# Expert weights stored in pairs and loaded a pair at a time, and the residual's rows loaded straight into their tiles

## The chip, the cores and the metric

The kernel runs on one core of a Trainium2 chip. The metric is device time in microseconds (us) from one run of the whole program; smaller is better. The core's engines are named as in the profile: PE (TensorE, matrix products), PEld (its weight loads), DVE (VectorE), ACT (ScalarE), POOL (GpSimd), SP (SyncE, which here issues nearly all DMAs). SPq in a row is the SP queue that issues DMAs.

## The reference

A small network on 512 tokens of width 1024, all in fp32: a transformer layer with attention and an MLP, a recurrent layer with an MLP, and a third layer with a token mixer and a mixture of experts. The change touches the end of it:

```python
x = x + g1 * token_mixer(h, ...)             # ends with merged @ w_out
h = rms_norm(x, norm2_g) * (1.0 + sc2) + sh2
x = x + g2 * hier_moe(h, ...)                # 32 experts, each token takes 2
return rms_norm(x, final_g)
# one expert on a block of tokens:
(silu(xb @ w_gate[e]) * (xb @ w_up[e])) @ w_down[e]      # 1024 -> 256 -> 1024
```

All 32 experts' weights are read whatever the routing is: 32 x 6 pieces ("units") of 128 x 1024 fp32, 512 KB each, 100.7 MB.

## The kernel before

**Stages.** The program runs the layers one after the other. Weights of the dense layers come through the tile pool `wr` (5 tiles of 512 KB) and are split into a high and a low part in the pool `wh` (4 tiles of 1 MB). A pool of 44 tiles of 128 x 512 (256 KB, `s2`) serves everything else. The last two stages matter here. `output_and_route` multiplies the merged token mixer `M` by `w_out` (the tiles `wo`; the second half of `w_out` stays in the four `wh` tiles `W` until token tile t = 3 is done), adds the residual, normalises (`norm`), writes the rows to DRAM (`h2d`, token tiles 0 to 2 from POOL, t = 3 from SP), and finds each token's experts (`pick`, `table`, `to_index`, which writes `idx`). `experts` then runs 17 blocks: 16 blocks `b` that hold 64 rows of expert b and 64 rows of expert b + 16, and one block "x" of 128 rows for the first expert with more than 64 tokens. For each block POOL gathers the rows (`xg<-h2d,idx`), PE transposes them (`xT`), multiplies by the gate and up weights (`gu`, units 0 to 3 of the expert) and by the down weights (`y`, units 4 and 5), and POOL scatters the result to DRAM (`yd`). At the end the results are read back (`yl`) and added.

**The ring.** Expert weights are loaded ahead into a ring of 33 units that reuses every free buffer: 4 units in own tiles (`wx`, 512 KB), 5 in `wr` tiles, 16 in pairs of `s2` tiles, 8 in the four `wh` tiles. A unit in one piece is one DMA with rows of 4 KB (line 2272); a unit in two `s2` tiles is two DMAs of 256 KB, "halves", with rows of 2 KB (line 2275). `ahead(n)` issues the next n units; `next_w` hands out a unit and calls `ahead(1)`. The calls before the first block are `ahead(4)`, `ahead(8)`, `ahead(9)` and `ahead(12)`. A load waits until the last reader of its buffer is done. All these loads stand in one in-order SP queue, in the order of the ring. Each DMA of the SP queue signals one of eight semaphores in turn and waits for the DMA eight places before it, so that at most eight are in flight.

**The residual.** The rows of the residual lie in DRAM (`xtok`). In `output_and_route` they are loaded to eight `s2` tiles `xt` (line 1860); `residual` multiplies `wo` by the gate into the old tiles `h` and adds `xt`.

```python
if x is not None:
    load = queue.dma_start(out=x, in_=src)                      # L2272: 128 x 1024
else:
    for h in range(2):
        load = queue.dma_start(out=halves[h], in_=src[:, h * 512:(h + 1) * 512])   # L2275: 128 x 512
```

Of the kernel before, what the change touches and what calls it, by code (L numbers as in the profile page):

```python
# [10 lines left out]
F32 = mybir.dt.float32  # L11
F32R = mybir.dt.float32r
# [3 lines left out]
ALU = mybir.AluOpType  # L16
# [4 lines left out]
NT = 4  # L21
# [23 lines left out]
class K:  # L45
# [1412 lines left out]
    def token_mixer(self, X):  # L1458
        nc, A = self.nc, self.A
# [32 lines left out]
        qt, kt, V, kcv = {}, {}, {}, {}  # L1492
# [318 lines left out]
    def open_moe(self):  # L1811
        nc = self.nc
        self.ctxb.close()
        self.c1 = self.ctx.enter_context(self.tc.tile_pool(name="c1", bufs=1))
        self.xg = [self.c1.tile([128, 1024], F32, name=f"xg{i}") for i in range(2)]
        for x in self.xg:
            nc.gpsimd.memset(x, 0.0)
        self.last_add = None
        self.raw, self.unit, self.last_load, self.pair = deque(), 0, None, None


        self.blocks = list(range(13)) + ["x"] + list(range(13, 16))

        def units(b, us):
            return [("x", u) for u in us] if b == "x" else [96 * j + 6 * b + u for u in us for j in range(2)]
# [24 lines left out]
    def output_and_route(self, M):  # L1850

        nc, A = self.nc, self.A
        self.moe_consts()
        g1 = self.row_bcast(self.modrow[0:1])
        self.router()
        xt = {}
        for g in range(2):
            for t in range(NT):
                xt[g, t] = self.s2("xt")
                nc.sync.dma_start(out=xt[g, t], in_=self.xtok[t, :, g * 512:(g + 1) * 512])  # L1860
        self.x2 = self.h
# [20 lines left out]
        for kb in range(4):  # L1882
            w = self.load_w(A["w_out"][0, kb], 1024)
# [258 lines left out]
    def block_rows(self, ov, idx, weight, sel=None):  # L2142


        nc = self.nc
        V = nc.vector
        pos, flag, wf = self.t([128, 8], "ovp"), self.t([128, 8], "ovm"), self.t([128, 2], "ovw")
        V.tensor_scalar(out=pos, in0=self.pe, scalar1=ov[:, 1:2], scalar2=None, op0=ALU.subtract)
        V.tensor_scalar(out=wf[:, 0:1], in0=ov[:, 0:1], scalar1=-1.0, scalar2=None, op0=ALU.add)
        V.tensor_scalar(out=flag, in0=self.ek, scalar1=wf[:, 0:1], scalar2=None, op0=ALU.is_equal)  # L2150
        V.tensor_scalar(out=wf[:, 0:1], in0=wf[:, 0:1], scalar1=0.0, scalar2=1536.0, op0=ALU.max, op1=ALU.mult)
        V.scalar_tensor_tensor(out=idx[:, 2:3], in0=self.io128, scalar=2.0, in1=wf[:, 0:1], op0=ALU.mult, op1=ALU.add)
# [12 lines left out]
        self.to_index(ps[:, 0:2], idx[:, 0:2])  # L2165
        self.shares(ps[:, 2:4], weight)
# [62 lines left out]

        return rows, first, turn, second  # L2230

    def unit_tile(self, m, name="wx"):

        m %= self.NWX + self.NWR + self.NWY + 2 * self.NWH
        if m < self.NWX:
            x = self.c1.tile([128, 1024], F32, name=name, tag="wx", bufs=self.NWX)
        elif m < self.NWX + self.NWR:
            x = self.wp.tile([128, 1024], F32, name=name, tag="wr", bufs=self.NWR)
        elif m < self.NWX + self.NWR + self.NWY:
            return None, [self.s2(name) for _ in range(2)]  # L2240
        else:
            n = (m - self.NWX - self.NWR - self.NWY) % 2
            if n == 0:
                self.pair = self.wp.tile([128, 2, 1024], F32R, name="wh", tag="wh", bufs=self.NWH).bitcast(F32)
            x = self.pair[:, n]
        return x, [x[:, 0:512], x[:, 512:1024]]

    def unit_rows(self, idx, u, halves):

        for h in range(2):  # L2250
            self.nc.gpsimd.indirect_dma_start(out=halves[h], out_offset=None,
                                              in_=self.A["moe_w"].rearrange("u p (h c) -> (u p h) c", h=2),
                                              in_offset=bass.IndirectOffsetOnAxis(ap=idx, axis=0),
                                              element_offset=u * 128 * 1024 + h * 512)
        return halves

    def ahead(self, n, queue=None):

        queue = queue or self.nc.sync
        for _ in range(n):  # L2260
            if self.unit == len(self.order):
                return
            u, (x, halves) = self.order[self.unit], self.unit_tile(self.unit)
            self.raw.append(halves)
            self.unit += 1
            if isinstance(u, tuple):
                self.unit_rows(self.xidx[:, 2:3], u[1], halves)
                continue
            src = self.A["moe_w"][u]
            with self.tc.issue_after(self.last_load) if self.last_load is not None else nullcontext():  # L2270
                if x is not None:
                    load = queue.dma_start(out=x, in_=src)  # L2272
                else:
# [4 lines left out]
    def next_w(self):  # L2278
        w = self.raw.popleft()
        self.ahead(1)  # L2280
        return w
# [20 lines left out]
    def experts(self):  # L2302
        nc, A, tc = self.nc, self.A, self.tc
# [13 lines left out]
        for b in self.blocks:  # L2317
            p = 16 if b == "x" else b
            row = self.xidx[:, 1:2] if b == "x" else self.idx[:, 16 + p:17 + p]
            done = (lambda y: last.update(y=y)) if b == self.blocks[-1] else (lambda y, row=row: put(row, y))  # L2320
            T.append(self.block_tasks(xg[len(T) % 2], ((0, 128),) if b == "x" else ((0, 64), (64, 128)),
                                      self.share[:, p:p + 1], self.next_w, done, len(T) >= n - 2))

        def fetch(i):
            b = self.blocks[i]
# [147 lines left out]
        nc.sync.dma_start(out=self.h[c], in_=self.A["xT"][c])  # L2473

    def run(self):
        self.NS2, self.NWR, self.NWH, self.NWX, self.NWY = 44, 5, 4, 4, 16
        self.AHEAD = 2
        self.open()
        self.open_a()
# [41 lines left out]
def layout(inp):  # L2521
# [129 lines left out]
```

## Time and profile before

| | us |
|---|---|
| median of 3 runs | 2326.76 (2326.37 to 2333.84) |
| the profiled execution, its own time | 2335.61 |
| its span, first to last instruction | 2333.8 |
| PE busy | 2193.7 (94%) |
| DVE busy | 1287.8 (55%) |
| ACT busy | 941.1 (40%) |

The profiled execution took 8.85 us longer than the median, and 1.8 us of its time lie outside its span. Shares over the whole span say little about the two last stages: the stretch from 2010 us to the end is read by windows, by the SP queue's timeline and by waits.

### The profile page before, as it was taken

To read this page: it belongs to the slowest core of one execution; us is meant where nothing else is said; L and a number is where in the kernel's file an instruction comes from. 1 tells how busy PE (TensorE), PEld (TensorE's weight loads), DVE (VectorE), ACT (ScalarE), POOL (GpSimd) and SP (SyncE) were. 2 spreads that over 40 slices of the span, in tenths; PEclk is the share of its full clock that TensorE was granted. 3 is DMA by queue.
4 is the path that set the end of the run, shared out by engine and by line. 5 is a ranking of instruction groups with operands and counts; after the bars stand their busy time and mean duration, and the time that the engine had idled before them with its cause. 6 is when DMAs were issued, how large, how long until landed. Compare 5 with 4: busy or idle time off the path is not lost.

```text
span 2333.8 us, 32061 instructions
## 1 busy us (share of the span) xinstructions
PE 2193.7 (94%) x12050; PEld 1707.5 (73%) x12050; DVE 1287.8 (55%) x2341; ACT 941.1 (40%) x1788; POOL 365.1 (16%) x390
## 2 busy tenths in 40 slices
PE   7999989999998999899999999899999999799886
PEld 5887887866888877878888899787878878633232
DVE  7566487564449779572444476614366655433224
ACT  5445653323234457453322345225257762311111
POOL 4001006122005132210000031200400001111211
PEclk9999999999999999999999999999999999799998
DMA  5211255654333421352223323654620015899996
GB/s 184 65 59 55 96 186 175 208 171 156 127 99 115 140 73 59 98 194 88 99 92 135 100 65 110 208 150 153 230 67 28 2 52 196 285 381 392 375 348 243
DMA packets 153045, 353.52 MB, mean 151 GB/s; under 512 B 31809, under 2 KB 43073, under 8 KB 152888
## 3 DMA queue, kind: packets, MB, share of 16 engines
q1 hardware_dynamic: 146696, 338.45, 42.8%
q0 software_dynamic: 6192, 13.00, 1.5%
q8 instruction: 96, 1.57, 0.3%
q14 instruction: 61, 0.50, 0.1%
HBM read 322.66 MB, written 39.84 MB: 155 GB/s over the span
## 4 chain that ended last, share of the span: by engine, by line
PE 50%; DMA 7%; DVE 6%; ACT 2%; issue 2%; SPq 1%; POOL 0%; ACTq 0%; DVEq 0%; POOLq 0%
PE mm L206 24%; PE mm L232 7%; PE gu L2193 3%; DMA wx<-in_moe_w_dram 3%; PE wo L1868 2%; PE O L1758 2%; PE S L533 2%; PE PT L587 2%; DMA wh<-in_moe_w_dram 2%; PE y L2193 1%; DVE wh L167 1%; PE mm L209 1%; DVE xc L907 1%; PE hps L1607 1%; SPq L1302 1%
## 5 line engine op out<-in xcount | busy, mean ns | idle before, releaser
L167 DVE TENSOR_TENSOR wh<-wr,wh 128x1024 fp32r<-128x1024 f32 x262 | 335.8, 1284 | 437.5 <-ACT wh L164 424.1
L164 ACT CAST wh<-wr 128x1024 fp32r<-128x1024 f32 x274 | 286.9, 1049 | 543.4 <-PE mm L206 394.5
L206 PE MATMUL mm<-xmh,wh 128*128 128x512 f32 x896 | 287.0, 398 | 12.1 <-ACT relu L386 12.1
L206 PE MATMUL mm<-hidh,wh 128*128 128x512 f32 x896 | 287.1, 399 | 4.0 <-DVE m L399 2.1
L206 PEld LDWEIGHTS mm<-xmh,wh 128*128 128x128 f32 x896 | 169.6, 190 | 53.6 <-ACT relu L386 15.6
L206 PEld LDWEIGHTS mm<-hidh,wh 128*128 128x128 f32 x896 | 168.9, 189 | 46.5 <-ACT wh L164 2.5
L206 PE MATMUL mm<-hidl,wh 128*128 128x512 f32 x448 | 179.4, 400 | 0.0
L206 PE MATMUL mm<-xml,wh 128*128 128x512 f32 x448 | 177.6, 396 | 0.0
L206 PE MATMUL mm<-x2h,wh 128*128 128x512 f32 x512 | 168.0, 400 | 2.4 <-ACT cmpY L1481 1.6
L631 PE MATMUL mm<-x0h,wh 128*128 128x512 f32 x384 | 128.3, 404 | 12.5 <-ACT wh L164 9.6
L2193 PE MATMUL gu<-wx,xT 128*64 128x512 f32 (+1 forms) x412 | 120.0, 621 | 13.6 <-DMA wx<-in_moe_w_dram 9.7
L206 PEld LDWEIGHTS mm<-x2h,wh 128*128 128x128 f32 x512 | 96.3, 189 | 22.4 <-ACT cmpY L1481 2.7
L2226 DVE SCALAR_TENSOR_TENSOR y<-y,share,g 128x512 f32<-128x512 f32 x34 | 25.4, 750 | 144.7 <-PE y L2193 136.5
L568 ACT ACTIVATE P<-S,nm 128x128 f32<-128x128 f32 (+3 forms) x192 | 100.5, 535 | 9.6 <-DVE nm L563 9.4
L267 POOL TENSOR_TENSOR sq<-sq 128x512 f32<-128x512 f32 x12 | 17.9, 1488 | 541.5 <-ACT sq L259 541.2
L206 PE MATMUL mm<-x2l,wh 128*128 128x512 f32 x256 | 101.8, 398 | 0.0
L232 PE MATMUL mm<-xgh,wh 128*128 128x256 f32 x512 | 96.4, 288 | 4.6 <-DVE wh L167 4.6
L206 PEld LDWEIGHTS mm<-hidl,wh 128*128 128x128 f32 x448 | 84.9, 189 | 20.7 <-issue 2.8
L206 PEld LDWEIGHTS mm<-xml,wh 128*128 128x128 f32 x448 | 85.1, 190 | 19.4 <-issue 2.3
L631 PEld LDWEIGHTS mm<-x0h,wh 128*128 128x128 f32 x384 | 73.0, 191 | 28.7 <-ACT wh L164 9.6
L2193 PEld LDWEIGHTS gu<-wx,xT 128*64 128x64 f32 (+1 forms) x412 | 32.9, 143 | 80.3 <-issue 44.4
L590 ACT COPY PTs<-PT 128x512 f32<-128x512 f32 (+3 forms) x128 | 63.5, 528 | 63.1 <-PE PT L587 62.6
(551 smaller groups left out, 4807.7 us busy)
## 6 DMA issues: line engine op xcount, KB each, us to landing
wx<-in_moe_w_dram SPq DMA_DIRECT2D x186, 256.0 KB
wr<-in_mlp_up_dram SPq DMA_DIRECT2D x64, 512.0 KB
wr<-in_mlp_down_dram SPq DMA_DIRECT2D x64, 512.0 KB
wx<-in_moe_w_dram SPq DMA_DIRECT2D x52, 512.0 KB
wr<-in_ada_w_dram SPq DMA_DIRECT2D x48, 512.0 KB
wh<-in_moe_w_dram SPq DMA_DIRECT2D x47, 512.0 KB
wr<-in_win_dram SPq DMA_DIRECT2D x40, 512.0 KB
wr<-in_attn_w_dram SPq DMA_DIRECT2D x24, 512.0 KB
```

The source lines that it names most:

```text
L164: nc.scalar.copy(out=wh[:, 0, cs], in_=w)
L167: (lo or nc.vector).tensor_tensor(out=wh[:, 1, cs], in0=w, in1=wh[:, 0, cs].bitcast(F32), op=ALU.subtract)
L206: nc.tensor.matmul(out=ps[j], lhsT=wh[:, b, o:o + 128], rhs=X[k][a], start=st, stop=sp)
L232: mm = nc.tensor.matmul(out=out, lhsT=keep[kb][:, b, o:o + 128], rhs=X[k][a][:, HALF[hf]], start=(k == 0 and n == 0 and j % 2 == 0), stop= ...
L533: nc.tensor.matmul(out=ps, lhsT=q[:, qs], rhs=part[:, 0:N], start=part is k[0], stop=False)
L568: nc.scalar.activation(out=p[:, ns], in_=ps[:, ns], func=AF.Exp, bias=nm[:, o + n:o + n + 1], accum_out=ss[:, o + n:o + n + 1])
L587: nc.tensor.transpose(out=pt[:, c:c + 128], in_=blk[:, kb * 128:(kb + 1) * 128], identity=self.ident)
L590: nc.scalar.copy(out=sb[:, 0:len(part) * N], in_=pt[:, 0:len(part) * N])
L631: nc.tensor.matmul(out=ps, lhsT=w[:, b, k * 128:(k + 1) * 128], rhs=X[k][a], start=(k == 0 and n == 0), stop=(k == 7 and n == 2))
L1758: nc.tensor.matmul(out=oo(e), lhsT=V[kb][:, tp * 256 + g * 64:tp * 256 + (g + 1) * 64], rhs=T[2 * m + e][kb], start=False, stop=(tp == 1 a ...
L1868: nc.tensor.matmul(out=ps, lhsT=M[k][a][:, t * 128:(t + 1) * 128], rhs=w[:, b, kk:kk + 512], start=(k == 0 and n == 0), stop=(k == 7 and n ...
L2193: nc.tensor.matmul(out=out[a:b], lhsT=x[:, c * 128 + a:c * 128 + b], rhs=u[n], start=start, stop=stop)
```

## The change

The weights lie in DRAM as 96 pairs: piece u of expert e and of expert e + 16 side by side, so that a partition's row of a pair is 8 KB. The ring counts in pairs and has 17 (34 units). Where the room is one piece of 1 MB (two new `wx` tiles, the four `wh` tiles) a pair is one DMA; a pair in two `wr` tiles is two DMAs with rows of 4 KB, a pair in four `s2` tiles is four with rows of 2 KB, and the pair called `mix` takes one `wr` and two `s2` tiles. All three read from rows of 8 KB now. The order of the ring is written out. The residual's rows are loaded straight into the tiles `h` (now `x2`), right behind the last use of `h` in `token_mixer`; `residual` writes the product to an `s2` tile `gated` and adds it. The eight `xt` tiles and their loads go. In the block "x" the row index is worked out with two more small DVE operations.

```diff
@@ token_mixer
         self.drain(self.soon)
+        self.x2 = self.h
+        for g in range(2):
+            for t in range(NT):
+                nc.sync.dma_start(out=self.x2[2 * t + g], in_=self.xtok[t, :, g * 512:(g + 1) * 512])
@@ output_and_route
-        xt = {}
-        for g in range(2):
-            for t in range(NT):
-                xt[g, t] = self.s2("xt")
-                nc.sync.dma_start(out=xt[g, t], in_=self.xtok[t, :, g * 512:(g + 1) * 512])
...
             x = self.x2[2 * t + g]
-            nc.vector.tensor_tensor(out=x, in0=ps, in1=g1[g], op=ALU.mult)
-            nc.vector.tensor_tensor(out=x, in0=x, in1=xt[g, t], op=ALU.add)
+            y = self.s2("gated")
+            nc.vector.tensor_tensor(out=y, in0=ps, in1=g1[g], op=ALU.mult)
+            nc.vector.tensor_tensor(out=x, in0=x, in1=y, op=ALU.add)
...
-        self.ahead(self.NWX)
+        self.ahead(2)
...
-        self.ahead(self.NWR + 3)
+        self.ahead(5)
...
-                self.ahead(9)
+                self.ahead(8)
             norm(t)
...
-        self.ahead(self.NWY - 12 + 2 * self.NWH)
+        self.ahead(len(self.RING) - 15)
@@ the ring
+    RING = ("wx",) * 2 + ("wr",) * 2 + ("s2",) * 3 + ("wh",) * 4 + ("s2",) * 5 + ("mix",)
...
+        if kind in ("wx", "wh"):
+            pool, bufs, dt = (self.c1, 2, F32) if kind == "wx" else (self.wp, self.NWH, F32R)
+            x = pool.tile([128, 2, 1024], dt, name=kind, tag=kind, bufs=bufs)
+            x = x if dt == F32 else x.bitcast(F32)
+            return [(x, slice(0, 2), slice(0, 1024))], [[x[:, j, 0:512], x[:, j, 512:1024]] for j in range(2)]
+        for j in range(2):
+            if kind == "wr" or (kind, j) == ("mix", 0):
+                x = self.wp.tile([128, 1024], F32, name="wr", tag="wr", bufs=self.NWR)
+                parts.append((x, j, slice(0, 1024)))
...
+            else:
+                halves.append([self.s2("wx") for _ in range(2)])
+                parts.extend((x, j, slice(h * 512, (h + 1) * 512)) for h, x in enumerate(halves[-1]))
@@ ahead
-            src = self.A["moe_w"][u]
+            src = self.A["moe_w"][6 * b + u]
...
-                if x is not None:
-                    load = queue.dma_start(out=x, in_=src)
-                else:
-                    for h in range(2):
-                        load = queue.dma_start(out=halves[h], in_=src[:, h * 512:(h + 1) * 512])
+                for x, j, cs in parts:
+                    load = self.nc.sync.dma_start(out=x, in_=src[:, j, cs])
@@ layout
-    A["moe_w"] = w.reshape(192, 128, 1024)
+    A["moe_w"] = np.ascontiguousarray(w.reshape(2, 96, 128, 1024).transpose(1, 2, 0, 3))
```

What the change does to the order of the SP queue is seen in three places.

The first is the end of `output_and_route`, up to the load of `g`. `wx`, `wr` and `wh` from `in_moe_w_dram` are expert weights, the size is that of the tile, `h2d` is the write of the rows of t = 3, `g` a gate row. Before:

```order
L1860 DMA xt<-xtok 128x512 x8
L2272 DMA wx<-in_moe_w_dram 128x1024 x4
L2275 DMA wx<-in_moe_w_dram 128x512 x24
L1908 DMA h2d<-h_17936 128x512
L1908 DMA h2d<-h_17937 128x512
L2275 DMA wx<-in_moe_w_dram 128x512 x8
L2272 DMA wh<-in_moe_w_dram 128x1024 x8
L2332 DMA g_18055<-modrow 128x1024
```

Now:

```order
L2282 DMA wr<-in_moe_w_dram 128x1024 x3
L2282 DMA wx<-in_moe_w_dram 128x512 x12
L2282 DMA wh<-in_moe_w_dram 128x2048 x4
L2282 DMA wx<-in_moe_w_dram 128x512 x16
L1908 DMA h2d<-h_17946 128x512
L1908 DMA h2d<-h_17947 128x512
L2282 DMA wx<-in_moe_w_dram 128x512 x4
L2282 DMA wr<-in_moe_w_dram 128x1024
L2282 DMA wx<-in_moe_w_dram 128x512 x2
L2347 DMA g_18051<-modrow 128x1024
```

The `xt` loads are gone. The four `wh` loads, which can start only as the matmuls of t = 3 release the second half of `w_out`, have moved from behind the `h2d` write to before it, and sixteen halves stand between them and the write.

The second is the stage before, where the residual's rows are loaded now (`h` tiles; `cw` are weights of another part). Before:

```order
L1591 DMA cw_14184<-in_cmp_w_dram 128x512
L1591 DMA cw_14186<-in_cmp_w_dram 128x512
L153 DMA wr<-in_win_dram 128x1024 x7
L153 DMA wr<-in_nsa_wo_dram 128x1024
L1620 DMA w_14302<-in_cmp_w_dram 128x256
```

Now:

```order
L1595 DMA cw_14184<-in_cmp_w_dram 128x512
L1595 DMA cw_14186<-in_cmp_w_dram 128x512
L1548 DMA h_86<-xtok 128x512
L1548 DMA h_93<-xtok 128x512
L1548 DMA h_100<-xtok 128x512
L1548 DMA h_107<-xtok 128x512
L1548 DMA h_91<-xtok 128x512
L1548 DMA h_98<-xtok 128x512
L1548 DMA h_105<-xtok 128x512
L1548 DMA h_109<-xtok 128x512
L153 DMA wr<-in_win_dram 128x1024 x7
```

Eight loads of 256 KB stand before the seven loads of `win`.

The third is the end of the loads (`ovd` is a write of a list, `fg` and `yl` serve the last sum). Before:

```order
L2275 DMA wx<-in_moe_w_dram 128x512 x22
L2138 DMA ovd<-ov 128x14x2
L2275 DMA wx<-in_moe_w_dram 128x512 x10
L2272 DMA wh<-in_moe_w_dram 128x1024 x8
L2417 DMA fg<-in_final_g_dram 128x512 x2
L2424 DMA yl<-yd 128x512 x16
```

Now:

```order
L2282 DMA wx<-in_moe_w_dram 128x512 x12
L2282 DMA wh<-in_moe_w_dram 128x2048
L2138 DMA ovd<-ov 128x14x2
L2282 DMA wh<-in_moe_w_dram 128x2048 x3
L2282 DMA wx<-in_moe_w_dram 128x512 x12
L2432 DMA fg<-in_final_g_dram 128x512 x2
L2439 DMA yl<-yd 128x512 x16
```

Behind `ovd` stood ten halves and eight units in `wh`; now three pairs in `wh` and twelve halves. The last three pairs, the last block's, come in rows of 2 KB, where they came in rows of 4 KB.

## Rows read from the trace of the kernel before

**Rows 1.** The page: the span; GB/s in 40 slices; one issue row, last column us to landing.

```profile
span 2333.8 us, 32061 instructions
...
GB/s 184 65 59 55 96 186 175 208 171 156 127 99 115 140 73 59 98 194 88 99 92 135 100 65 110 208 150 153 230 67 28 2 52 196 285 381 392 375 348 243
...
h2d<-h POOLq DMA_DIRECT2D x6, 256.0 KB, 2.9
```

**Rows 2.** Busy time, then TensorE clock, DMA share and GB/s, by stretch.

```profile
1990.00:2010.00 20.00, 20.00 (x121) 17.24 (x120) 5.98 (x20) 8.36 (x20) 2.44 (x4) 1.00 0.61 203
2010.00:2020.00 10.00, 8.14 (x45) 6.91 (x43) 6.11 (x38) 5.74 (x13) 1.08 (x2) 0.90 0.97 363
2020.00:2030.00 10.00, 2.64 (x11) 2.37 (x11) 8.26 (x52) 1.05 (x3) 1.10 (x1) 0.50 0.94 292
...
2044.00:2292.00 248.00, 224.56 (x940) 79.66 (x936) 75.19 (x203) 38.82 (x97) 41.07 (x41) 0.97 1.01 373
2270.00:2280.00 10.00, 10.00 (x48) 3.17 (x46) 2.80 (x6) 1.17 (x4) 0.07 (x1) 1.00 0.77 125
```

**Rows 3.** The same in four 5 us windows of the expert stage.

```profile
2065.00:2070.00 5.00, 4.71 (x22) 1.63 (x24) 2.06 (x10) 1.07 (x3) 0.00 (x0) 1.00 1.04 389
...
2095.00:2100.00 5.00, 5.00 (x25) 1.66 (x22) 1.49 (x3) 0.00 (x0) 0.00 (x0) 1.00 1.03 409
...
2165.00:2170.00 5.00, 4.51 (x17) 1.25 (x16) 0.00 (x0) 0.00 (x0) 0.00 (x0) 1.00 0.89 277
...
2225.00:2230.00 5.00, 1.96 (x7) 0.47 (x6) 0.00 (x0) 0.00 (x0) 0.00 (x0) 0.96 0.93 320
```

**Rows 4.** Timeline of the SP queue: start, us, line, DMA, count.

```profile
1965.64 5.07 SPq L1860 DMA_DIRECT2D xt<-xtok  x8
...
1986.79 28.71 SPq L2275 DMA_DIRECT2D wx<-in_moe_w_dram  x24
2018.85 0.94 SPq L1908 DMA_DIRECT2D h2d<-h  x2
2019.88 5.96 SPq L2275 DMA_DIRECT2D wx<-in_moe_w_dram  x8
2025.90 5.33 SPq L2272 DMA_DIRECT2D wh<-in_moe_w_dram  x8
...
2042.37 8.55 SPq L2272 DMA_DIRECT2D wx<-in_moe_w_dram  x9
```

**Rows 5.** Timeline of the other engines around the first gather.

```profile
2008.69 0.48 PE L1868 MATMUL wo<-wh,Ml 128*128 128x512 f32 x1
...
2014.33 0.40 PE L1868 MATMUL wo<-wh,Mh 128*128 128x512 f32 x1
...
2027.58 0.19 DVE L2099 TENSOR_SCALAR idx<-tab 128x32 int32<-128x32 f32 x1 [0.54 <-PE tab L2086]
...
2028.62 1.10 POOL L2284 DMA_INDIRECT xg<-h2d,idx  x1 [14.82 <-DMA wx<-in_moe_w_dram]
...
2037.10 1.94 PE L2179 MATMUL xT<-ident,xg 128*128 128x128 f32 x8 [5.23 <-DMA xg<-h2d,idx]
...
2038.97 6.38 PE L2193 MATMUL gu<-wx,xT 128*64 128x512 f32 x22
```

**Rows 6.** Waits of the SP queue, 1900 to 2334: us in total, times, longest.

```profile
SPq L2275 <- DMA wx<-in_moe_w_dram: 73.6, 121, 2.8
...
SPq L2272 <- PE gu L2193: 15.4, 10, 8.8
```

**Rows 7.** The chain that ended last: start, us, what.

```profile
2283.22 9.15 DMA wh<-in_moe_w_dram
...
2300.43 5.98 DMA yl<-yd
```

**Rows 8.** Timeline of SP, then of ACT, in the stage where the new loads stand.

```profile
1666.00 25.59 SPq L153 DMA_DIRECT2D wr<-in_win_dram  x7
...
1683.47 1.05 ACT L164 CAST wh<-wr 128x1024 fp32r<-128x1024 f32 x1 [0.89 <-PE mm L206]
```

More of the change, by code (lines that the diff above doesn't have):

```diff
@@ L1818, in open_moe @@
         self.last_add = None
-        self.raw, self.unit, self.last_load, self.pair = deque(), 0, None, None
+        self.raw, self.unit, self.last_load = {}, 0, None
         self.blocks = list(range(13)) + ["x"] + list(range(13, 16))
         def units(b, us):
-            return [("x", u) for u in us] if b == "x" else [96 * j + 6 * b + u for u in us for j in range(2)]
+            return [(b, u) for u in us if b != "x" or u % 2 == 0]
         self.order = units(self.blocks[0], range(4))
@@ L2150, in block_rows @@
         V.tensor_scalar(out=flag, in0=self.ek, scalar1=wf[:, 0:1], scalar2=None, op0=ALU.is_equal)
-        V.tensor_scalar(out=wf[:, 0:1], in0=wf[:, 0:1], scalar1=0.0, scalar2=1536.0, op0=ALU.max, op1=ALU.mult)
-        V.scalar_tensor_tensor(out=idx[:, 2:3], in0=self.io128, scalar=2.0, in1=wf[:, 0:1], op0=ALU.mult, op1=ALU.add)
+        V.tensor_scalar(out=wf[:, 1:2], in0=wf[:, 0:1], scalar1=16.0, scalar2=-49150.0, op0=ALU.is_ge, op1=ALU.mult)
+        V.tensor_scalar(out=wf[:, 0:1], in0=wf[:, 0:1], scalar1=0.0, scalar2=3072.0, op0=ALU.max, op1=ALU.mult)
+        V.tensor_tensor(out=wf[:, 0:1], in0=wf[:, 0:1], in1=wf[:, 1:2], op=ALU.add)
+        V.scalar_tensor_tensor(out=idx[:, 2:3], in0=self.io128, scalar=4.0, in1=wf[:, 0:1], op0=ALU.mult, op1=ALU.add)
         yield
@@ L2230, in block_tasks, with pair_tiles @@
         return rows, first, turn, second
[L2232 to L2240, printed above, removed]
-        else:
[L2242 to L2246, printed above, removed]
+    RING = ("wx",) * 2 + ("wr",) * 2 + ("s2",) * 3 + ("wh",) * 4 + ("s2",) * 5 + ("mix",)
+    def pair_tiles(self, m):
+        kind = self.RING[m % len(self.RING)]
+        if kind in ("wx", "wh"):
[3 more added lines that the diff above has]
+            return [(x, slice(0, 2), slice(0, 1024))], [[x[:, j, 0:512], x[:, j, 512:1024]] for j in range(2)]
+        parts, halves = [], []
+        for j in range(2):
+            if kind == "wr" or (kind, j) == ("mix", 0):
+                x = self.wp.tile([128, 1024], F32, name="wr", tag="wr", bufs=self.NWR)
+                parts.append((x, j, slice(0, 1024)))
+                halves.append([x[:, 0:512], x[:, 512:1024]])
+            else:
+                halves.append([self.s2("wx") for _ in range(2)])
+                parts.extend((x, j, slice(h * 512, (h + 1) * 512)) for h, x in enumerate(halves[-1]))
+        return parts, halves
     def unit_rows(self, idx, u, halves):
@@ L2251, in unit_rows, with ahead @@
             self.nc.gpsimd.indirect_dma_start(out=halves[h], out_offset=None,
-                                              in_=self.A["moe_w"].rearrange("u p (h c) -> (u p h) c", h=2),
+                                              in_=self.A["moe_w"].rearrange("q p j (h c) -> (q p j h) c", h=2),
                                               in_offset=bass.IndirectOffsetOnAxis(ap=idx, axis=0),
-                                              element_offset=u * 128 * 1024 + h * 512)
+                                              element_offset=u * 128 * 2048 + h * 512)
         return halves
-    def ahead(self, n, queue=None):
-        queue = queue or self.nc.sync
+    def ahead(self, n):
         for _ in range(n):
@@ L2262, in ahead, with loader, load @@
                 return
-            u, (x, halves) = self.order[self.unit], self.unit_tile(self.unit)
-            self.raw.append(halves)
+            (b, u), (parts, halves) = self.order[self.unit], self.pair_tiles(self.unit)
             self.unit += 1
-            if isinstance(u, tuple):
-                self.unit_rows(self.xidx[:, 2:3], u[1], halves)
+            for j in range(2):
+                self.raw[(b, u + j, 0) if b == "x" else (b, u, j)] = halves[j]
+            if b == "x":
+                for j in range(2):
+                    self.unit_rows(self.xidx[:, 2:3], u + j, halves[j])
                 continue
-            src = self.A["moe_w"][u]
+            src = self.A["moe_w"][6 * b + u]
             with self.tc.issue_after(self.last_load) if self.last_load is not None else nullcontext():
-                if x is not None:
-                    load = queue.dma_start(out=x, in_=src)
-                else:
-                    for h in range(2):
-                        load = queue.dma_start(out=halves[h], in_=src[:, h * 512:(h + 1) * 512])
-            self.last_load = load.ins
[L2278 to L2281, printed above, removed]
+                for x, j, cs in parts:
+                    load = self.nc.sync.dma_start(out=x, in_=src[:, j, cs])
+            self.last_load = load.ins
+    def loader(self, b):
+        keys = iter([(b, u, j) for u in range(6) for j in range(1 if b == "x" else 2)])
+        def load():
+            key = next(keys)
+            w = self.raw.pop(key)
+            if (key[1] if b == "x" else key[2]) % 2:
+                self.ahead(1)
+            return w
+        return load
     def gather(self, xg, idx):
@@ L2321, in experts @@
             T.append(self.block_tasks(xg[len(T) % 2], ((0, 128),) if b == "x" else ((0, 64), (64, 128)),
-                                      self.share[:, p:p + 1], self.next_w, done, len(T) >= n - 2))
+                                      self.share[:, p:p + 1], self.loader(b), done, len(T) >= n - 2))
         def fetch(i):
@@ L2475, in run @@
     def run(self):
-        self.NS2, self.NWR, self.NWH, self.NWX, self.NWY = 44, 5, 4, 4, 16
+        self.NS2, self.NWR, self.NWH = 44, 5, 4
         self.AHEAD = 2
```

1 line of the change is left out of this document (removed).

## The prediction

> **What bounds the kernel now.** I read the page's slices first: the GB/s climb from 28, 2 and 52 through 196 and 285 to 381, 392, 375 and 348, so the end is another regime than the rest [rows 1]. Then windows by stage: from 2044 to 2292 us the DMA engines' share is 1.01 at 373 GB/s, while PE, though busy for 224.6 of 248 us, only follows [rows 2]. The SP queue's waits say what holds the loads: 73.6 us in 121 waits of halves for earlier weight DMAs, but only 15.4 us for the products that free their buffers, 8.8 of them in one wait [rows 6]. So from the moment the full ring is first released (2042.37, [rows 4]) the loads run back to back, and the chain of waits ends on them: the last wait for a `wh` weight starts at 2283.22, then comes the read of `yl` [rows 7]. There is one hole, 2270 to 2280, share 0.77 at 125 GB/s, where the list `ovd` goes out [rows 2]. A change pays here if it (a) restarts that stream earlier, (b) has more in the ring at the restart, or (c) raises the rate. What happens before 2044 counts only through (a) and (b).
>
> **What sets the restart.** The first gather waits for the expert index and for the whole of `h2d`. The index is there at 2027.58, the gather goes out at 2028.62, PE transposes at 2037.10 and multiplies from 2038.97, and SP reuses the first buffer at 2042.37 [rows 4, 5]. The `h2d` write of t = 3 was issued at 2018.85; two of the halves behind it reuse its semaphores and wait for its end, and the `wh` loads behind them start at 2025.90 [rows 4]. So the write had landed by then, before the index: the index was late, not the write.
>
> **The restart, step by step.** Now the write stands behind four `wh` pairs and sixteen halves. The 24 matmuls of t = 3 run from 2008.69 to 2014.73 [rows 5] and release `W` by quarters: about 2010.4, 2012, 2013.3 and 2014.7. The queue is blocked until the first. Then 4 x 1.05 MB, 16 x 0.26 MB and the write's 0.52 MB, 8.9 MB, pass before the write is done. At 409 GB/s ([rows 3], units in one piece) that is 21.8 us, at 363 ([rows 2], the stretch where this now happens) 24.5. A lone 256 KB write from POOL takes 2.9 us to land [rows 1], of which at 400 GB/s some 0.7 is data, so 2.2 us come on top. The write lands between 2034.4 and 2037.1; I take the middle, 2035.7, since the first half of these bytes is large pieces and the rest halves. The gather then leaves at about 2035.9, 7.3 us later than now (bounds 5.8 and 8.5). Its 8.5 us to the transposes and the 5.3 us from there to the first release stay. The restart moves to about 2049.7: **+7.3 us**. The cover is gone here: while the write was hidden behind the index it cost nothing.
>
> The Trainium skill, "DMA: Bandwidth & Descriptors", section "Queues, rings and completion order", says that on each DMA engine descriptors are consumed in ring order. That is what makes the write wait; the trace agrees as far as the write, with up to six halves ahead of it, took under 7.1 us against 2.9 for one from POOL's queue.
>
> **What the ring holds then.** Before the block the ring now ends in the order above; the DMA engines idle between the twelve early halves (which wait only for products long done, and go out from about 1986.8, where the halves do now) and 2010.4. In the kernel before they ran at share 0.61 from 1990 to 2010 [rows 2]. By 2010 that is 14 units against about 16.5, but from 2010.4 the queue has 20 units and the write, about 13 MB with two gathers and `g`; at 400 GB/s it is done at about 2044, before the restart. So the arrears cost nothing, and the ring is full with 34 units instead of 33: 0.52 MB at 389 GB/s, **-1.35 us**.
>
> **The rate.** After the restart come 164 units (86 MB). Of them 28 pairs, 29.4 MB, come in rows of 8 KB instead of 4; the number of halves stays (156 for 154). Windows give 389 GB/s for a run of halves and 409 for units in one piece [rows 3], 2.571 and 2.445 us per MB. If a row's own cost makes the difference, doubling the row saves 0.126 per MB from 2 to 4 KB and 0.063 from 4 to 8: **-1.85 us**. No trace shows 8 KB rows; the bounds are 0 (the engines are at their ceiling at 409) and twice that step, -3.7. The halves now stand in runs of 12 and of 20 (and 2 in `mix`), not of 32. Late in a run of 32 the rate falls to 277 and 320 at shares of 0.89 and 0.93 [rows 3]: there the engines are not kept full, since SP waits for the eighth DMA before, and eight halves are 2 MB only. If shorter runs did away with a 10 us stretch at 300 in place of 389 in each of four rounds, 9 us would come back; if nothing changes, 0. I take **-2 us**, nearer to nothing, since more than half of the halves still stand ninth or later in their run. The last 3.1 MB become halves: **+0.4 us**.
>
> **What costs nothing.** The eight `xt` loads (2.1 MB, 5 us of the queue at 1965.64, [rows 4]) go, in a stretch whose loads are waited for by nobody yet. Their eight successors stand before seven loads of `win`; they cost about 5.5 us of transfer, and the first of the seven goes out at 1666.00 while its cast comes at 1683.47 [rows 8], since five earlier tiles are used first. Without that slack it would be 5.5 us. `residual` has the same two DVE operations; the two new ones of 128 x 1 stand outside any wait.
>
> **The sum.** 7.3 - 1.35 - 1.85 - 2 + 0.4 = +2.5 us, on the profiled execution's 2335.61 (span 2333.8 plus 1.8 around it): 2338.1. The median of the runs shown is 8.85 lower; I move it by the same 2.5 to **2329**. About 0.3% (7 us) is what a measurement of this kernel can tell from no change.
>
> **Rivals.**
> 1. *The stream becomes faster.* The write is issued earlier than I think or the large pieces run so fast that it lands with the index (then 0 instead of +7.3), and shorter runs give more. With the upper bounds of the rate: 0 - 1.35 - 3.7 - 4 + 0.4 = -8.7, **2318**. For it: the shares under 1 late in the runs. Against: 4 MB in `wh` cannot start before 2010.4, and nothing before the change overtakes them. The Trainium skill, "DMA: Bandwidth & Descriptors", section "Measured", advises batches of 1 MiB and more for over 75% of peak; by its 425 GB/s for large transfers, an estimate, the 29.4 MB would save 2.7 us. The trace shows 409 with 512 KB pieces, so most of that advantage is there already.
> 2. *The late write is all there is.* Same place, but the halves behind the `wh` pairs run at 300 GB/s, as halves did around 2020 to 2030 (292, [rows 2]), so that the write lands at 2039: 8.9 MB as 4.2 at 409 and 4.7 at 300 is 26 us, plus 2.2. The gather moves by 10, and 8 KB rows bring nothing: 10 - 1.35 + 0.4 = +9, **2336**. It decides (slower by over 7) once the write lands later than about 2036.6 with no gain in rate. For it: the small rate where halves and writes meet. Against: some gain of rate is likely.
> 3. *It doesn't move at all*, because gather and restart are bound by something else by then (the products of t = 3, the table): -1.35 - 1.85 and no more, **2324**. This falls within 0.3%.
>
> **Numbers.** Forecast, net within 7 us by the sum: 0.42; rival 3: 0.10; rival 1: 0.20; rival 2: 0.28. So faster by over 0.3%: 0.20; within 0.3%: 0.52; slower by over 0.3%: 0.28. The range reaches from rival 1 to past rival 2: 2317 to 2341; the forecast's own is 2322 to 2333.
>
> **What would show it.** Right: SP issues the `h2d` write of t = 3 after 2024 instead of 2018.85; DMA share near 0 from about 1995 to 2010; the first gather 6 to 8 us after the index; a DMA gap of some 5 us before the restart; thereafter windows around 415 to 420 in `wh` stretches and fewer windows below 350. Wrong: a gather within 2 us of the index; a PE or DVE wait in the `gated` products; windows in `wh` stretches at 409 as before and a last weight that lands 6 us later; or PE, not the loads, ending the chain.

## The result, and the profile after

The changed kernel takes 2339.11 us (median of 6 runs, 2335.93 to 2342.05), the kernel before 2326.07 beside it (6 runs): a ratio of 1.0053, 95% interval 1.004 to 1.0065. It is slower by 12 to 13 us. The profiled execution took 2339.75 us, its span is 2337.9.

The timeline of the SP queue, which answers to [rows 4] (start, us, line, DMA, count):

```profile
1976.56 7.68 SPq L2282 DMA_DIRECT2D wx<-in_moe_w_dram  x12
2008.94 4.97 SPq L2282 DMA_DIRECT2D wh<-in_moe_w_dram  x4
2014.00 16.56 SPq L2282 DMA_DIRECT2D wx<-in_moe_w_dram  x16
2030.96 1.00 SPq L1908 DMA_DIRECT2D h2d<-h  x2
2032.27 2.35 SPq L2282 DMA_DIRECT2D wx<-in_moe_w_dram  x4
...
2049.96 2.36 SPq L2282 DMA_DIRECT2D wx<-in_moe_w_dram  x2
```

The write of t = 3 (`h2d`) goes out at 2030.96, behind the four `wh` pairs and sixteen halves. The ring restarts at 2049.96. The other engines around the first gather, which answer to [rows 5]: the index, the gather, the transposes and the first products.

```profile
2026.59 0.19 DVE L2099 TENSOR_SCALAR idx<-tab 128x32 int32<-128x32 f32 x1 [0.54 <-PE tab L2086]
2037.74 1.10 POOL L2299 DMA_INDIRECT xg<-h2d,idx  x1 [25.35 <-DMA h2d<-h]
2044.37 1.94 PE L2182 MATMUL xT<-ident,xg 128*128 128x128 f32 x8 [13.48 <-DMA xg<-h2d,idx]
2046.24 5.71 PE L2196 MATMUL gu<-wx,xT 128*64 128x512 f32 x16
```

The gather waits for the write (the releaser in brackets is `h2d<-h`) and goes out 11.2 us after the index; in [rows 5] it was 1.0. The windows of the stretch, answering to [rows 2] (length, busy time of PE, PEld, DVE, ACT, POOL, then granted clock, DMA share, GB/s):

```profile
1980.00:1985.00 5.00, 3.95 (x12) 3.11 (x13) 4.86 (x9) 2.13 (x6) 0.00 (x0) 0.71 0.91 311
1985.00:1990.00 5.00, 5.00 (x26) 4.11 (x25) 1.26 (x2) 1.72 (x5) 0.00 (x0) 0.94 0.73 275
1990.00:2000.00 10.00, 10.00 (x60) 8.58 (x59) 2.59 (x7) 5.77 (x12) 1.37 (x2) 1.00 0.14 53
2000.00:2010.00 10.00, 10.00 (x64) 8.84 (x63) 4.38 (x23) 3.67 (x11) 1.08 (x2) 1.00 0.20 61
2010.00:2020.00 10.00, 7.07 (x40) 6.08 (x38) 5.68 (x34) 5.84 (x10) 1.08 (x2) 0.81 0.93 338
2020.00:2030.00 10.00, 3.62 (x15) 3.36 (x15) 7.41 (x47) 0.31 (x2) 0.00 (x0) 0.50 1.03 400
2030.00:2040.00 10.00, 0.89 (x5) 0.78 (x4) 0.35 (x2) 0.00 (x0) 1.95 (x2) 0.50 1.02 375
2040.00:2045.00 5.00, 0.63 (x3) 0.66 (x4) 0.00 (x0) 0.00 (x0) 0.17 (x1) 0.50 0.73 284
2045.00:2050.00 5.00, 5.00 (x17) 2.15 (x17) 1.58 (x4) 3.00 (x5) 0.99 (x1) 0.50 0.29 79
2050.00:2055.00 5.00, 5.00 (x24) 1.40 (x20) 0.00 (x0) 0.00 (x0) 0.00 (x0) 0.96 0.78 301
2055.00:2060.00 5.00, 4.83 (x26) 1.92 (x24) 2.06 (x5) 2.17 (x5) 0.99 (x1) 1.00 0.85 280
```

Two things stand there. The DMA engines are nearly idle from 1990 to 2010 (0.14 and 0.20), then full, and then they run dry again: from 2040 to 2060 the four shares 0.73, 0.29, 0.78 and 0.85 leave 5 x (0.27 + 0.71 + 0.22 + 0.15) = 6.75 us of engine time unused. And PE is busy for only 3.95 of the 5 us from 1980, at a mean clock of 0.71. DVE and PE at that place:

```profile
1979.08 1.23 DVE L167 TENSOR_TENSOR wh<-wr,wh 128x1024 fp32r<-128x1024 f32 x1 [2.96 <-ACT wh L164]
1980.22 0.68 DVE L1873 TENSOR_TENSOR gated<-wo,rowb 128x512 f32<-128x512 f32 x1
...
1977.52 0.40 PE L1867 MATMUL wo<-wh,Mh 128*128 128x512 f32 x1
1981.05 0.47 PE L1867 MATMUL wo<-wh,Mh 128*128 128x512 f32 x1 [3.13 <-DVE gated L1873]
...
1982.39 1.05 PE L1867 MATMUL wo<-wh,Mh 128*128 128x512 f32 x2
...
1986.82 0.63 PE L1867 MATMUL wo<-wh,Mh 128*128 128x512 f32 x2
```

The first `gated` product stands on DVE behind the split of the last quarter of `w_out`; that split waits for ACT's copy, which waits for a `wh` buffer that PE frees only with its last product of the first half. So PE waits 3.13 us for the `gated` product, which reads out the PSUM tile (where PE's sums lie) that PE writes next. Afterwards a pair of matmuls takes 1.05 us until about 1985, later 0.63: the granted clock is at the lower of its two levels (1.2 instead of 2.4 GHz) from about 1982.1 on, behind the wait (2.1 us at 1.0 and 2.9 at 0.5 give the window's 0.71), and the next window's 0.94 puts its end at 1985.6. That is 3.5 us at half speed, 1.75 lost; with the wait 4.9. In the kernel before, three splits stood ahead of the first product and the fourth (L167) behind it, and PE did not wait:

```profile
1982.06 1.28 DVE L1873 TENSOR_TENSOR h<-wo,rowb 128x512 f32<-128x512 f32 x2
...
1985.12 1.23 DVE L167 TENSOR_TENSOR wh<-wr,wh 128x1024 fp32r<-128x1024 f32 x1
```

The waits of the SP queue from 1900 us on, answering to [rows 6], and the end of the chain that ended last, answering to [rows 7]:

```profile
SPq L2282 <- DMA wx<-in_moe_w_dram: 79.4, 139, 3.2
SPq L2282 <- PE gu L2196: 21.9, 18, 12.4
```

```profile
2279.24 13.67 DMA wh<-in_moe_w_dram
...
2303.09 5.76 DMA yl<-yd
```

The loads still end the program. The largest wait for a product is 12.4 us now (8.8 before): SP stands still at the restart.

### The profile page after: what moved, and what is told of

It reads as the page before. It is cut to its first block, busy times and chain, and to the rows that moved or that the text cites. A ratio compares the mean times of both kernels' runs of the same rounds, so it can differ in the third digit from the quotient of the medians.

```text
span 2337.9 us, 32004 instructions
## 1 busy us (share of the span) xinstructions
PE 2179.7 (93%) x12050; PEld 1700.7 (73%) x12050; DVE 1288.3 (55%) x2343; ACT 943.4 (40%) x1788; POOL 366.8 (16%) x390
## 5 line engine op out<-in xcount | busy, mean ns | idle before, releaser
L167 DVE TENSOR_TENSOR wh<-wr,wh 128x1024 fp32r<-128x1024 f32 x262 | 333.5, 1275 | 438.2 <-ACT wh L164 434.6
L206 PE MATMUL mm<-xmh,wh 128*128 128x512 f32 x896 | 286.9, 398 | 12.4 <-ACT relu L386 12.4
L2229 DVE SCALAR_TENSOR_TENSOR y<-y,share,g 128x512 f32<-128x512 f32 x34 | 25.5, 750 | 137.3 <-PE y L2196 123.6
L2196 PE MATMUL gu<-wx,xT 128*64 128x512 f32 x340 | 91.0, 616 | 5.5 <-DMA wx<-in_moe_w_dram 5.0
L206 PE MATMUL mm<-xrh,wh 128*128 128x512 f32 x256 | 82.7, 396 | 4.8 <-DVE xrr L969 3.7
```

Of the source, the lines that this page charges most:

```text
L167: (lo or nc.vector).tensor_tensor(out=wh[:, 1, cs], in0=w, in1=wh[:, 0, cs].bitcast(F32), op=ALU.subtract)
L206: nc.tensor.matmul(out=ps[j], lhsT=wh[:, b, o:o + 128], rhs=X[k][a], start=st, stop=sp)
L2196: nc.tensor.matmul(out=out[a:b], lhsT=x[:, c * 128 + a:c * 128 + b], rhs=u[n], start=start, stop=stop)
L2229: nc.vector.scalar_tensor_tensor(out=y[:, s], in0=ps[h], scalar=weight, in1=self.g2[:, s], op0=ALU.mult, op1=ALU.mult)
```

## The experiments

In the expectations, theory A is the late write, B the larger unit in which a pair's buffer comes free, C the stall of PE at 1978 us, D the place of the rows in DRAM. Ratios are to the kernel before, with 95% intervals; 0.001 is 2.3 us.

### The write of t = 3 from POOL (e1_pool), and the old order of the ring (e2_ring)

```diff
-                (nc.gpsimd if t < 3 else nc.sync).dma_start(out=self.h2d[t * 128:(t + 1) * 128, g * 512:(g + 1) * 512], in_=h2[g])
+                nc.gpsimd.dma_start(out=self.h2d[t * 128:(t + 1) * 128, g * 512:(g + 1) * 512], in_=h2[g])
```

> The changed kernel, with the rows of t = 3 written by POOL like those of the other token tiles, so that the write no longer stands in the SP queue behind four wh pairs and sixteen halves. Theory A (the late write holds the first gather): the gather goes out within 2 us of the index (about 2028 us instead of 2037.7), the restart of the ring comes some 8 to 9 us earlier (about 2041 instead of 2049.96), and the median falls from 2339.1 by 7 to 9 us to 2330 to 2332. Theory B (what costs is that a pair's buffer comes free only when both its units are read, so that the DMA engines run part empty after the restart whenever it comes): the restart moves as above, but the stretch of low DMA share behind it stays, and the median falls by 3 us at most, to 2336 or more.

```diff
-    RING = ("wx",) * 2 + ("wr",) * 2 + ("s2",) * 3 + ("wh",) * 4 + ("s2",) * 5 + ("mix",)
+    RING = ("wx",) * 2 + ("wr",) * 2 + ("s2",) * 8 + ("mix",) + ("wh",) * 4
...
-                self.ahead(8)
+                self.ahead(6)
...
-        self.ahead(len(self.RING) - 15)
+        self.ahead(len(self.RING) - 13)
```

> The changed kernel with its pairs in the order of the kernel before: wx, wr, all s2 pairs, mix, and the four wh pairs last; the write of t = 3 stays with SP but stands behind the halves only, ahead of the wh pairs. Sizes, rows and DMAs per pair are unchanged. Theory A: the write goes out at about 2018 us, the gather follows the index, the DMA engines are busy again between 1990 and 2010 us, and the median falls by 7 to 9 us to 2330 to 2332. Theory B: at most 3 us, 2336 or more. If instead the shorter runs of halves have given much, the longer run of 32 halves takes it back and the median stays above 2334.

Measured: 2335.48 us, 1.0035 (1.0025 to 1.0045), and 2335.27, 1.0041 (1.0026 to 1.0056). Both lie between A and B. In the trace of e1_pool A's mechanism is complete: the gather follows the index by 1.4 us, and the restart comes at 2039.34.

```profile
2025.70 0.19 DVE L2099 TENSOR_SCALAR idx<-tab 128x32 int32<-128x32 f32 x1 [0.54 <-PE tab L2086]
2027.06 1.10 POOL L2299 DMA_INDIRECT xg<-h2d,idx  x1 [7.96 <-DVE half L2046]
```

The DMA engines have a share of 1.02 from 2040 to 2050 and 1.04 after, so B falls: with the restart earlier there is no hole behind it, though pairs come free as before.

```profile
2040.00:2050.00 10.00, 9.83 (x50) 3.56 (x48) 2.06 (x5) 2.48 (x6) 0.99 (x1) 1.00 1.02 413
2050.00:2060.00 10.00, 9.58 (x50) 3.64 (x46) 2.49 (x17) 1.35 (x4) 1.45 (x2) 1.00 1.04 394
```

In the trace of e2_ring the gather goes out at 2028.93, still 3.0 us behind the index. In both runs only 4 us of the 12 to 13 are gone.

### The split held back (e4_split)

```diff
-        W = [self.load_w(A["w_out"][1, kb], 1024) for kb in range(4)]
+        W = [self.load_w(A["w_out"][1, kb], 1024) for kb in range(3)]
+        wr3 = self.wp.tile([128, 1024], F32, name="wr", tag="wr", bufs=self.NWR)
+        nc.sync.dma_start(out=wr3, in_=A["w_out"][1, 3])
...
-            residual(ps[t], 0, t)
+            r = residual(ps[t], 0, t)
+            if t == 1:
+                with self.tc.issue_after(r.ins):
+                    W.append(self.split_w(wr3, 1024))
```

> The changed kernel with the split of the last quarter of the second half of w_out (DVE and ACT) held behind the residual of t = 1, as it stood in the kernel before; loads and writes are unchanged. In the changed kernel this split stands ahead of the first gated product, and PE waits 3.1 us for it at 1978 us and then runs 2 us at a granted clock of 0.5. Theory C (this stall is in series with the late write): PE goes on without a wait, everything behind comes 3 to 5 us earlier, median 2334 to 2336. Against it: if the stall is covered by something that the gather waits for anyway, the median stays at 2339 within 1 us.

Measured: 2337.06, 1.0043 (1.003 to 1.0056). PE has no wait there any more. By itself the edit brings 2 us, which these intervals do not tell from nothing.

### Rows of 4 KB in the same order (e3_rows4)

```diff
-            return [(x, slice(0, 2), slice(0, 1024))], [[x[:, j, 0:512], x[:, j, 512:1024]] for j in range(2)]
+            return [(x[:, j], j, slice(0, 1024)) for j in range(2)], [[x[:, j, 0:512], x[:, j, 512:1024]] for j in range(2)]
```

> The changed kernel with the same order and the same tiles, but each pair in wx and wh is loaded by two DMAs of 128 x 1024 (rows of 4 KB) instead of one of 128 x 2048 (rows of 8 KB). By the prediction's term for the rows the time rises by 1.85 us (bounds 0 and 3.7) to 2341; if the engines are at their ceiling with 4 KB rows already, it stays at 2339 within 1 us. Theory B expects a small gain (1 to 3 us, 2336 to 2338) if the two halves of a pair's buffer can be filled one after the other.

Measured: 2346.55, 1.0084 (1.0071 to 1.0097): 7 us more than the changed kernel (about 3 to 11 by the two intervals), four times the prediction's term. B expected a gain and falls here as well. If the long rows gain so much, other parts must cost more than the write and the stall had shown alone; the next runs ask for them in the kernel before.

### Parts of the change in the kernel before (b1_layout, b2_resid, b3_pool)

The layout, with the ring and the DMAs of before. The edit also has the index arithmetic of the block "x" that goes with the layout, two more small DVE operations (left out below), so it is not the place of the rows alone:

```diff
-            src = self.A["moe_w"][u]
+            src = self.A["moe_w"][u % 96, :, u // 96]
...
-    A["moe_w"] = w.reshape(192, 128, 1024)
+    A["moe_w"] = np.ascontiguousarray(w.reshape(2, 96, 128, 1024).transpose(1, 2, 0, 3))
```

> The kernel before, with the weights stored by pairs in DRAM and nothing else: the same ring of 33 units, the same DMAs of 128 x 1024 and 128 x 512, which now read 4 KB or 2 KB out of rows that lie 8 KB apart. After the first four runs some 8 to 10 us of the change's 13 are still without a cause: without the late write it is 2335.5, without the DVE stall 2337.1, while with rows of 4 KB it is 2346.6. Theory D (pieces cut out of wider rows come more slowly): slower than before by 5 to 10 us, 2332 to 2337. Against it: the place of the rows in DRAM is of no account, 2327 within 1.5 us.

The residual part alone is the diff's hunks in `token_mixer` and `residual`, and `xt` gone:

> The kernel before with the residual part of the change alone: rows loaded into the tiles h in token_mixer, product into an s2 tile called gated, no xt tiles. Layout and ring as before. Theory C: if the order on DVE comes out as in the changed kernel, PE waits 3 us at about 1978 us and the restart comes as much later, 2329 to 2331; if the order stays as before, 2327 within 1.5 us. A cost of the eight loads ahead of the win loads (5.5 us by the prediction if they are not covered) would show here too, in the time of the first expert load, 1910 to 1915 us in the runs so far.

The control has e1_pool's edit:

> The kernel before with the rows of t = 3 written by POOL: the control for the same edit on the changed kernel, and a second trace of the kernel before. The write was hidden behind the index there, so theory A expects no change, 2327 within 1.5 us, and a first gather within 2 us of the index. If POOL's queue is itself the better way for the write, it gains as on the changed kernel, 3 us or more.

Measured: layout 2329.13, 1.0017 (1.0006 to 1.0028); residual 2330.09, 1.0014 (1.0002 to 1.0026); control 2327.1, 1.0001 (0.9991 to 1.0012). The layout edit costs something, 1.4 to 6.5 us, which is below most of what D asked for. The residual part alone brings the same stall: in its trace PE waits 3.13 us for `gated` at 1980.39, and the index comes at 2025.04 us, 5 us later than in the control when both are counted from the first expert load.

```profile
1980.39 0.77 PE L1866 MATMUL wo<-wh,Mh 128*128 128x512 f32 x1 [3.13 <-DVE gated L1872]
```

Its eight early loads show no cost: that first load is at 1908.97 us there and at 1909.89 in the control, and in the traces with these loads it lies between 1908.09 and 1915.63, in those without them between 1909.89 and 1915.45. The write from POOL brings nothing where it was hidden already.

The control is also a better trace of the kernel before than the one in the rows above, whose profiled execution stood 8.85 us over the median; there the first expert load was at 1915.45 already, so most of that excess lay ahead of this stage.

### Both edits (c1_both)

> The changed kernel with both edits: the rows of t = 3 written by POOL, and the split of the last quarter of w_out held behind the residual of t = 1. If the late write (3.6 us) and the stall (2.0 us) add, 2333 to 2334. If they overlap (the stall no longer holds up the gather once the write is out of the way, or the other way round), 2335 as with the write alone.

Measured: 2327.77, 1.0004 (0.9991 to 1.0016). The two edits together take back all of it, as far as the interval tells (2.1 us under the kernel before to 3.7 over), and more than the sum of the medians (3.6 and 2.0), though not more than their intervals allow. At the restart the traces add up. Each time here is counted from the first expert load of its own trace, less the same in the control:

| us later than the control | index | gather | restart | read of `yl` | end of span |
|---|---|---|---|---|---|
| kernel before, trace of the rows above | 1.0 | 1.0 | 2.9 | 2.6 | 3.1 |
| changed kernel | 5.4 | 15.5 | 15.8 | 11.0 | 12.6 |
| e1_pool (stall left) | 4.5 | 4.9 | 5.2 | 4.2 | 5.5 |
| e2_ring (stall left, write behind the halves only) | 5.7 | 7.7 | 9.9 | 7.8 | 7.4 |
| e4_split (late write left) | 0.8 | 11.1 | 10.5 | 8.8 | 9.5 |
| c1_both | 0.1 | 0.1 | -0.2 | 0.8 | -0.1 |

For instance the restart of the changed kernel: (2049.96 - 1910.12) - (2033.93 - 1909.89) = 15.8. The first row has the order of the control and differs from it only in who writes t = 3, so up to 3 us lie between two such traces; and the profiled execution of e1_pool was 3 us faster than its median, so its last two columns may be too good by as much. The stall puts 5.2 us on the restart and the late write 10.5, in series, since the four `wh` pairs can start only when the delayed products of t = 3 release `W`. The control and c1_both, index, gather and restart:

```profile
2020.98 0.19 DVE L2099 TENSOR_SCALAR idx<-tab 128x32 int32<-128x32 f32 x1 [0.54 <-PE tab L2086]
2022.02 1.10 POOL L2284 DMA_INDIRECT xg<-h2d,idx  x1 [8.04 <-DVE half L2045]
...
2033.93 8.55 SPq L2272 DMA_DIRECT2D wx<-in_moe_w_dram  x9
```

```profile
2021.63 0.19 DVE L2104 TENSOR_SCALAR idx<-tab 128x32 int32<-128x32 f32 x1 [0.55 <-PE tab L2091]
2022.67 1.10 POOL L2304 DMA_INDIRECT xg<-h2d,idx  x1 [8.16 <-DVE half L2050]
...
2034.28 2.04 SPq L2287 DMA_DIRECT2D wx<-in_moe_w_dram  x2
```

### Order, rows and size of the large pieces, on c1_both (d1_inter, d2_ring, d3_rows4, d4_part64)

```diff
-    RING = ("wx",) * 2 + ("wr",) * 2 + ("s2",) * 3 + ("wh",) * 4 + ("s2",) * 5 + ("mix",)
+    RING = ("wx", "wx", "wr", "s2", "wr", "s2", "s2") + ("wh", "s2") * 4 + ("s2", "mix")
```

> The kernel with both edits (POOL writes t = 3, the split held back; 2327.8 us), and with its ring interleaved: after wx, wx come wr, s2, wr, s2, s2, then wh and s2 in turn four times, s2, mix. So the halves stand in runs of 4 or 8 (10 at the end) between large pieces instead of in runs of 12 and 20. The prediction's term for shorter runs (2 us, bounds 0 and 9) grows if it is right: the median falls by 2 to 5 us, to 2323 to 2326. If the order of large and small pieces is of no account, it stays within 1.5 us of 2327.8.

The edit of e2_ring on c1_both:

> The kernel with both edits and with the ring in the order of the kernel before (runs of 32 to 34 halves, the wh pairs last). By the term for shorter runs the median rises by 2 to 5 us over 2327.8, to 2330 to 2333; if the order is of no account it stays within 1.5 us. If the engines' idle time between 1990 and 2005 us, in which halves now can go, was worth something, it falls by 1 to 3 us.

The edit of e3_rows4 on c1_both:

> The kernel with both edits, each pair in wx and wh loaded by two DMAs of 128 x 1024 (rows of 4 KB, 512 KB each). In the changed kernel the same edit cost 7.4 us, four times the prediction's 1.85. If that is what such rows or such DMAs cost in this order of the ring, 2333 to 2336 here too; if it belonged to the late restart, 2328 to 2330.

```diff
-            return [(x, slice(0, 2), slice(0, 1024))], [[x[:, j, 0:512], x[:, j, 512:1024]] for j in range(2)]
+            return [(x[64 * n:64 * n + 64], slice(64 * n, 64 * n + 64), slice(0, 1024)) for n in range(2)], [[x[:, j, 0:512], x[:, j, 512:1024]] for j in range(2)]
```

> The kernel with both edits, each pair in wx and wh loaded by two DMAs of 64 partitions x 2048 (rows of 8 KB, 512 KB each). It tells the row from the DMA's size: if the length of the row makes the difference, 2328 within 1.5 us; if it is the bytes in a DMA (at most eight DMAs are in flight, so smaller ones mean fewer bytes in flight ahead of the halves), as d3, 2333 to 2336. Transfers to half of the partitions may have a cost of their own, which would show as a rate below 400 GB/s in the windows where such pairs run alone.

Measured: d1_inter 2328.04, 1.0003 (0.999 to 1.0016); d2_ring 2329.47, 1.001 (0.9999 to 1.0022); d3_rows4 2332.25, 1.0025 (1.0015 to 1.0036); d4_part64 2411.13, 1.0358 (1.0338 to 1.0379). The order of large and small pieces moves nothing that can be measured. Rows of 4 KB cost 0.0021 of the time, 4.9 us (about 1 to 9 by the two intervals), against c1_both. The last run doesn't decide between row and size, since it has a cost of its own. Windows in which large pieces run, of c1_both, of d3_rows4 and of d4_part64 (last columns: clock, DMA share, GB/s):

```profile
2065.00:2070.00 5.00, 3.86 (x22) 1.44 (x19) 2.37 (x5) 0.38 (x1) 0.62 (x1) 1.00 1.00 417
2090.00:2095.00 5.00, 5.00 (x24) 1.57 (x20) 1.86 (x4) 0.00 (x0) 0.08 (x1) 1.00 1.03 423
```

```profile
2080.00:2085.00 5.00, 5.00 (x26) 1.71 (x26) 0.26 (x1) 0.37 (x1) 0.00 (x0) 1.00 1.04 402
2125.00:2130.00 5.00, 4.72 (x26) 1.77 (x22) 3.72 (x10) 1.25 (x3) 2.04 (x2) 1.00 1.02 409
```

```profile
2080.00:2085.00 5.00, 5.00 (x26) 1.61 (x23) 2.04 (x4) 0.03 (x1) 0.72 (x1) 1.00 1.05 238
2160.00:2165.00 5.00, 2.28 (x8) 0.86 (x8) 0.00 (x0) 0.00 (x0) 0.00 (x0) 0.80 1.01 213
```

One DMA to all 128 partitions with 8 KB rows runs at 417 to 423 GB/s, two with 4 KB rows at 402 to 409, two that fill 64 partitions each at 213 to 238 with the engines just as busy. No version here is faster than the kernel before beyond what its interval leaves open.

## Where the prediction was right and where it was wrong

The forecast was 2329 and no measurable change; it came out at 2339.1 and slower. The stated range, 2317 to 2341, holds 2339.1, but by luck: it reached past rival 2 for a late write and rows that bring nothing, not for a stall of PE. Rival 2 has the nearest price (2336). Its mechanism was another: the halves behind the `wh` pairs did not run at 300 GB/s but at 400 (window 2020 to 2030). Its other half, that the long rows bring nothing, fits the mean rates below.

- **What bounds the kernel** was read rightly: the loads still end the chain, and what happens before the restart counts through the restart.
- **The restart, +7.3 us, was too small.** The mechanism is as foretold: the write after 2024, the idle engines from 1995 to 2010, the gather behind it, the DMA gap. The step that failed in size is "8.9 MB pass before the write is done", and with it the gather's 7.3 us. With the stall taken out (e4_split) the gather comes 11.1 us later than in the control, or 10.1 later than in the trace that the prediction read. From the first `wh` load to the gather 28.8 us pass, where the prediction had 25.5, and a window over just this stretch shows what moved in it: 28.8 us at 362 GB/s, 10.4 MB. By queue, 0.52 MB of that is POOL's write of the rows of t = 2 (q0). So about 1.0 MB of loads that were issued behind the write moved beside it, and bytes behind it in the queue have to be counted too. The rate from 2010 to 2020 is 338 GB/s, where the sum had 363 to 409.

```profile
2008.94:2037.74 28.80, 12.64 (x62) 11.05 (x60) 14.41 (x88) 6.51 (x15) 1.08 (x2) 0.63 0.98 362
```

```profile
q1 hardware_dynamic: 3681, 9.87, 93.2%
q0 software_dynamic: 160, 0.52, 4.5%
```

- **"Its 8.5 us to the transposes and the 5.3 us from there" stay** was wrong the other way: with the DMA engines running dry behind the gather, 6.6 us pass to the transposes (2037.74 to 2044.37). So the late write moves the restart by 10.5 us counted from the control and by 7.7 counted from the trace that the prediction read.
- **"`residual` has the same two DVE operations", at no cost, was wrong**, and the prediction never looked at where they stand. Same operations, another order: the fourth split went ahead of the first product. That is 5.2 us on the restart (e1_pool), and b2_resid shows it without the rest of the change. "A PE or DVE wait in the `gated` products" was among the signs that it would be wrong. What in the planning moved the split was not tried.
- **From the restart to the end the prediction carried the delay one to one.** Of 15.8 us at the restart 11.0 are left at the read of `yl`. An early restart finds the ring's last loads still under way (in c1_both the share is 1.05 from 2030 to 2040), a late one finds the engines empty: the 6.75 us unused between 2040 and 2060 are what it really loses there, beside what was lost between 1990 and 2010. That reading fits the shares; no run took it apart.
- **Ring and rate, -1.35 - 1.85 - 2 + 0.4 = -4.8 us, are not there.** c1_both, without the late write and the stall, stands between 2.1 us under the kernel before and 3.7 over. Mean rates of the expert stage say the same. In order: the kernel before, the control, the changed kernel, c1_both, b1_layout, e3_rows4.

```profile
2060.00:2260.00 200.00, 176.67 (x721) 62.03 (x717) 65.23 (x182) 29.91 (x76) 37.08 (x37) 0.97 1.02 383
2060.00:2260.00 200.00, 179.98 (x721) 63.09 (x717) 59.39 (x149) 28.75 (x72) 36.07 (x36) 0.97 1.01 380
2060.00:2260.00 200.00, 175.16 (x764) 61.86 (x762) 65.34 (x184) 31.62 (x78) 37.84 (x38) 0.99 1.01 383
2060.00:2260.00 200.00, 177.11 (x752) 61.90 (x750) 62.25 (x155) 31.72 (x79) 36.75 (x37) 0.97 1.01 379
2060.00:2260.00 200.00, 179.66 (x723) 62.38 (x720) 59.99 (x156) 28.92 (x73) 36.08 (x36) 0.97 1.01 380
2060.00:2260.00 200.00, 177.57 (x746) 61.45 (x744) 63.73 (x180) 30.57 (x76) 37.23 (x38) 0.98 1.01 376
```

- **8 KB rows, -1.85 us:** where large pieces run, the rate is as foretold (415 to 420; 417 and 423 measured), but the mean over the stage is no higher than with the rows of 4 KB in the kernel before (379 in c1_both and 383 in the changed kernel, against 383 and 380). What d3_rows4 and e3_rows4 price is another step: they have rows of 4 KB too, and are still slower than the kernel before (d3_rows4, without the late write and the stall, takes 1.0015 to 1.0036 of its time; e3_rows4 moves 376 GB/s). So their 4.9 and 7.2 us (0.0084 - 0.0053 of 2327) say what one large DMA saves over two in the new layout and ring, not what the change gained. Whether the row or the bytes in flight make that difference, and what uses up the faster stretches, stays open.
- **Shorter runs of halves, -2 us, was not seen**: 4 to 10, 12 and 20, or 34 in a run give 1.0003, 1.0004 and 1.001. The intervals, about 4 us for a difference, rule out the bound of 9 but not 2. Dips of the share remain in c1_both: 0.95 and 0.94 in the windows from 2075 to 2085 us, at 329 and 291 GB/s.
- **The new layout had no price in the sum.** b1_layout takes 1.4 to 6.5 us more than the kernel before. With 4.9 gained by the large DMAs, 4.0 lost by the layout (both from the ratios) and the 34th unit's 1.35, c1_both should stand 2.2 us under the kernel before, at the edge of its interval, so in times the books close only to within 3 us or so. The trace of b1_layout does not show where its time goes: the mean rate is the control's (380), and its restart comes 1.4 us behind the control's, less than the 2.9 between two traces of the old order. So it is not shown that pieces cut from wider rows come more slowly. The 34th unit and the block "x" were not tried apart.
- **The early residual loads** show no cost, as said: the first expert load stands at 1910.12 us, in the control at 1909.89.

## What to carry to other kernels

When loads are put ahead of others in an in-order queue, look for the small write that the next stage waits for: it should not stand behind megabytes of weights, and some of the loads behind it may move beside it (1.0 MB here). When an edit leaves an engine the same operations, still compare the order in which they stand there, since here a product that frees a PSUM tile stood behind a split that waited for PE, a stall of 3.1 us. Two delays in series may each look small when taken away alone, so take them away together before looking for a third cause. And a run that takes back one part of a change prices that part in the new kernel; compare its rate with the old kernel's before calling it a gain.

## What the runs showed of the hardware that was not expected

Two DMAs of 64 partitions with 8 KB rows move 213 to 238 GB/s at a DMA share of 1.01 to 1.05, half of what one DMA of 128 partitions moves, and the kernel takes 83 us longer (2411.13 - 2327.77). The Trainium skill, "SBUF — State Buffer", section "Can I just issue two DMAs to hit both halves?", says that two concurrent DMAs on the two halves of the partitions serialize, and that only one transfer over all 128 reaches all ports; the trace agrees. And a wait of 3.1 us on PE cost about 5 us at the index (5.4 in the changed kernel, 5.0 in b2_resid): the granted clock stood at its lower level for 3.5 us behind it.
